# Two-layer sliding-window attention with gated MLP: the attention items' start, period and transposes in a hand-scheduled kernel

## The chip, the cores and the metric

The kernel runs on one core of a Trainium2 chip. The metric is the device time of one execution in microseconds (us). Engines are named as in the profile: PE (TensorE matmuls), PEld (its weight loads), DVE (VectorE), ACT (ScalarE), POOL (GpSimd), SP (the queue that issues weight transfers).

## What is computed

Two blocks run one after the other on a sequence of 512 tokens of width 1024. The first block (a pooling mixer and a gated recurrence) is not touched. The second block has two equal layers, and the change lies in these. Cut to what matters, one layer is:

```
for l in range(DEPTH):                                   # 2 layers
    h = x @ w_in[l] + b_in[l]
    q, k, v, z_a, u_g, v_g, z_g, g_a, g_g = split_columns(h)
    y_a = sliding_window_attention(q, k, v, attn_sinks[l]) * silu(z_a)
    y_g = chunked_spatial_gating(gelu(u_g), gelu(v_g), ...) * silu(z_g)
    merged = sigmoid(g_a) * (y_a @ w_branch_attn[l]) + sigmoid(g_g) * (y_g @ w_branch_gmlp[l])
    x = layer_norm(ALPHA * x + merged @ w_out[l] + b_out[l], ...)

# sliding_window_attention: blocks of 128 queries, keys of this block and the one before
scores = q k^T / 8 - slope * dist, masked;  m = max(scores.max(-1), sink)
p = exp(scores - m);  out = (p / (p.sum(-1) + exp(sink - m))) @ v
```

## The kernel before

All tensors are in SBUF with features on the partitions, 512 tokens along the free axis. Each projection is made from 256-column units of a weight. A float32 product is done as three matmuls of rounded parts: `hi` (a rounded copy, made by ACT in line 239) and `lo` (the remainder, made by DVE in line 245), and likewise `xhi` and `xlo` of the activations; so one 128-feature tile of a projection is 8 x 3 matmuls of 128x512 into a PSUM tile `pi` (line 319 is the one line that issues every matmul, line 323 every transpose).

The whole program is put in order by hand, while it is built. The main thread issues projections; beside it stand jobs (Python generators, list `sides`). After every few matmuls the main thread calls `tick()`, which gives each job in the list one step: what a step issues goes into the engines' queues at that place. A job that yields a number of microseconds is left alone until a counter of planned PE time (`clock`) has passed by that much. The engines run their queues strictly in that order, and semaphores hold an instruction until its operands are there.

A layer goes: `layer_head` (projections of k, v and q, six PSUM tiles, two of them the two-bank tiles `pj` of which there are two buffers in all), then `layer` with the evacuation of these tiles (`ev_kv`, `ev_q`, lines 1346 to 1381), the units u0 and u1 (GELU, line 1400), vg (GELU and a layer norm per 128 tokens, lines 1620 to 1631), za0 and za1, zg0 and zg1 (SiLU by Tanh), `mix`, the gates, branches and the output.

Attention runs beside u, vg, za and zg. It is eight items (four query blocks n, two key/value heads g) of each four query heads. `attention` first forces everything in `need` to be issued (the evacuation of k, v and q), then spawns an item, gives it its first step, and waits `ATT` us before the next one:

```
def start(at):                                   # called with "u0", "u1", "vg0", ...
    if at == ATT_AT:
        z["att"] = self.spawn(self.attention(l, qs, ks, vtok, z, need))
...
job = self.spawn(self.att_item(l, n, g, qs, ks, vtok, z, prev))
self.step(job)
yield ATT
```

An item (`att_item`, from line 1676) is: 8 score matmuls on PE into a `pj` tile (out of `ks`, the keys, and `H`, which here is `qs`, the queries); bias, maximum (DVE, lines 1698 to 1708); Exp on ACT (line 1715); normalisation on DVE (lines 1719 to 1723); `yield self.after(t0, ATT_P)`, that is, a pause until `ATT_P` us after the scores; then four or eight 128x128 transposes on PE into another `pj` tile (their operand is called `s`, the normalised rows); rounded copies of the transposes (ACT line 1739, DVE line 1743); a pause of `ATT_O`; the product with the values (`vtok`, "PV" below) on PE; copy out (ACT line 1758). The queries come from DVE line 1381: eight subtractions, `H_1282` (g = 0) and `H_1283` (g = 1) in turn, each over 64 partitions, and item 0 (g = 0) reads all four of `H_1282`.

Of the kernel before, what the change touches and what calls it, by code (L numbers as in the profile page):

```python
# [27 lines left out]
QCH = 388  # L28
QBUFS = 4
P3_SLOTS = 9  # L30
ATT = 9
ATT_P = 12
ATT_O = 5
ATT_AT = "u1"
WAITS = {"za": (1, 0), "u": (1, 0), "zg": (1, 1)}
COLS = 3
CONSTS = 8
# [28 lines left out]
class Net:  # L66
# [1261 lines left out]
    def layer(self, l, xt, cols):  # L1328
# [78 lines left out]
        def start(at):  # L1407
            if at == ATT_AT:
                z["att"] = self.spawn(self.attention(l, qs, ks, vtok, z, need))
# [252 lines left out]
    def attention(self, l, qs, ks, vtok, z, need):  # L1662
# [4 lines left out]
        for n in range(4):  # L1667
            for g in range(2):
# [3 lines left out]
                self.step(job)  # L1672
                yield ATT
        return outs

    def att_item(self, l, n, g, qs, ks, vtok, z, prev):
# [44 lines left out]
        for j in range(4):  # L1721
            s = ph[j // 2][:, j % 2, :]
            nc.vector.tensor_scalar(s, s, rd[:, j:j + 1], None, op0=ALU.mult)  # L1723
        yield self.after(t0, ATT_P)
        pts = []
# [154 lines left out]
```

## Time and profile before

| | before |
|---|---|
| three runs, median (lowest to highest) | 1653.32 us (1653.0 to 1653.61) |
| the profiled execution, its own time | 1654.04 us |
| its span | 1652.3 us |
| PE busy | 1628.9 us, 99% |
| DVE busy | 997.3 us, 60% |
| ACT busy | 600.9 us, 36% |
| POOL busy | 111.0 us, 7% |
| DMA, mean | 85 GB/s |
| mean granted TensorE clock | 0.997 of full |

Start times are counted from the first instruction of the span; the own time of the profiled execution also holds 1.7 us that lie around the span. Layer 0 of the second block runs from about 980 to 1308 us, layer 1 from there to the end. A matmul's duration in the profile is longer than the distance to the next one's start, since they are pipelined: what a matmul costs a full PE is the distance from its start to the next start.

### The profile page before, as it was taken

How to read it: one execution, taken by the hardware profiler on the slowest of the kernel's cores; microseconds unless marked ns; L12 is line 12 of the kernel's file. 1: busy time of each engine (PE TensorE's matmuls, PEld its weight loads, DVE VectorE, ACT ScalarE, POOL GpSimd, SP SyncE). 2: the span in 40 equal slices, each digit the busy share in tenths (PEclk: the TensorE clock that was granted, in tenths of full speed). 3: DMA queues.
4: the chain of work that ended last, by engine and by line, in shares of the span. 5: the costliest groups of instructions: out<-in, count | busy, mean ns of one | idle time of the engine just before them, and what ended most of it. 6: DMA issues, size and time to landing. Idle time of an engine off the chain costs nothing.

```text
span 1652.3 us, 25936 instructions
## 1 busy us (share of the span) xinstructions
PE 1628.9 (99%) x10726; PEld 1474.2 (89%) x10726; DVE 997.3 (60%) x1879; ACT 600.9 (36%) x996; POOL 111.0 (7%) x171
## 2 busy tenths in 40 slices
PE   8999999999999999999999999999999999999997
PEld 7999999989999898888999898978888899788886
DVE  6564647466666757567666756686424656873346
ACT  4432222244322223223222236564223355752221
POOL 4000000031000000000000010011000200010002
PEclk9999999999999999999999999999999999999999
DMA  5323222222221221221211232132325232232231
GB/s 189 103 81 99 84 96 86 94 78 82 65 77 52 77 66 63 77 77 58 86 62 63 66 109 85 44 103 79 100 77 153 71 102 65 77 99 91 92 102 51
DMA packets 124776, 139.67 MB, mean 85 GB/s; under 512 B 5217, under 2 KB 109809, under 8 KB 124658
## 3 DMA queue, kind: packets, MB, share of 16 engines
q1 hardware_dynamic: 122178, 131.88, 25.4%
q0 software_dynamic: 2304, 5.81, 1.2%
q8 instruction: 84, 1.38, 0.3%
q14 instruction: 34, 0.28, 0.1%
q10 hardware_dynamic: 176, 0.33, 0.1%
HBM read 135.90 MB, written 2.10 MB: 84 GB/s over the span
## 4 chain that ended last, share of the span: by engine, by line
PE 90%; DVE 6%; ACT 2%; issue 1%; POOL 1%; DMA 0%; DVEq 0%; ACTq 0%; POOLq 0%
PE pj L319 56%; PE pi L319 31%; PE pi L323 2%; DVE lo L245 1%; PE pj L323 1%; DVE s L1698 0%; ACT pj L1555 0%; ACT s L1715 0%; DVE mx L1704 0%; DVE h1tok L1550 0%; POOL ss L1558 0%; DVE h1tok L1565 0%; DVE s L1743 0%; POOL rs L361 0%; DVE s L1723 0%
## 5 line engine op out<-in xcount | busy, mean ns | idle before, releaser
L245 DVE TENSOR_TENSOR lo<-raw,hi 128x1024 fp32r<-128x1024 f32 (+1 forms) x260 | 296.7, 1171 | 153.4 <-ACT hi L239 153.1
L319 PE MATMUL pj<-xhi,hi 128*128 128x264 f32 (+2 forms) x1360 | 347.6, 311 | 0.7 <-ACT xhi L482 0.7
L319 PE MATMUL pj<-xlo,hi 128*128 128x264 f32 (+2 forms) x1360 | 340.3, 306 | 5.2 <-DVE xlo L783 2.3
L319 PE MATMUL pj<-xhi,lo 128*128 128x264 f32 (+2 forms) x1360 | 339.4, 305 | 0.0
L239 ACT CAST hi<-raw 128x1024 fp32r<-128x1024 f32 (+1 forms) x260 | 247.2, 996 | 170.4 <-PE pj L319 94.0
L319 PEld LDWEIGHTS pj<-xlo,hi 128*128 128x128 f32 x1360 | 227.0, 190 | 14.6 <-DVE xlo L783 2.7
L319 PEld LDWEIGHTS pj<-xhi,hi 128*128 128x128 f32 x1360 | 228.1, 190 | 11.2 <-ACT xhi L482 1.1
L319 PEld LDWEIGHTS pj<-xhi,lo 128*128 128x128 f32 x1360 | 227.0, 190 | 10.4
L319 PE MATMUL pi<-xhi,hi 128*128 128x512 f32 (+3 forms) x576 | 213.1, 370 | 0.0
L319 PE MATMUL pi<-xhi,lo 128*128 128x512 f32 (+3 forms) x576 | 210.8, 366 | 0.0
L319 PE MATMUL pi<-xlo,hi 128*128 128x512 f32 (+3 forms) x576 | 210.6, 366 | 0.0
L319 PEld LDWEIGHTS pi<-xhi,lo 128*128 128x128 f32 x576 | 108.4, 188 | 17.5
L319 PEld LDWEIGHTS pi<-xhi,hi 128*128 128x128 f32 x576 | 108.5, 188 | 17.1
L319 PEld LDWEIGHTS pi<-xlo,hi 128*128 128x128 f32 x576 | 108.5, 188 | 16.6
L319 PE MATMUL pj<-s,hi 128*128 128x264 f32 x640 | 104.1, 284 | 0.0
L1106 DVE TENSOR_TENSOR s<-s,s 128x264 f32<-128x264 f32 (+1 forms) x112 | 47.8, 427 | 82.2 <-PE pi L319 81.3
L319 PEld LDWEIGHTS pi<-qq,s 128*32 128x32 f32 (+5 forms) x1024 | 87.2, 161 | 7.4 <-issue 4.0
L319 PE MATMUL pi<-qq,s 128*32 128x32 f32 (+5 forms) x1024 | 89.7, 245 | 0.0
L319 PEld LDWEIGHTS pj<-s,hi 128*128 128x128 f32 x640 | 88.9, 188 | 0.0
L319 PE MATMUL pj<-hi,yA 128*128 128x512 f32 x256 | 71.6, 401 | 0.5
L361 POOL TENSOR_TENSOR rs<-ms,cst 128x4 f32<-128x4 f32 (+2 forms) x27 | 23.4, 868 | 696.7 <-DVE ms L1223 537.5
L319 PE MATMUL pj<-s,lo 128*128 128x264 f32 x320 | 65.3, 285 | 0.0
(262 smaller groups left out, 2365.2 us busy)
## 6 DMA issues: line engine op xcount, KB each, us to landing
raw<-in_hgrn_w_in_dram SPq DMA_DIRECT2D x64, 512.0 KB, 3.8
raw<-in_w_in_dram SPq DMA_DIRECT2D x60, 512.0 KB, 3.7
raw<-in_pool_w_in_dram SPq DMA_DIRECT2D x32, 512.0 KB, 3.7
raw<-in_pool_w_out_dram SPq DMA_DIRECT2D x16, 512.0 KB, 3.8
raw<-in_hgrn_w_out_dram SPq DMA_DIRECT2D x16, 512.0 KB, 3.6
raw<-in_w_in_dram SPq DMA_DIRECT2D x32, 256.0 KB, 3.2
raw<-in_w_out_dram SPq DMA_DIRECT2D x16, 512.0 KB, 4.7
raw<-in_pool_w_grp_dram SPq DMA_DIRECT2D x8, 512.0 KB, 4.0
```

The costliest lines, as they stand in the source:

```text
L239: nc.scalar.copy(a, r)
L245: eng.tensor_tensor(b, r, a.bitcast(F32), op=ALU.subtract)
L319: self.nc.tensor.matmul(out, w, x, start=start, stop=stop)
L323: self.nc.tensor.transpose(out, x, ident)
L361: self.nc.gpsimd.tensor_tensor(y, x, self.mhalf[:m, :n], op=ALU.pow)
L1106: nc.vector.tensor_tensor(kv[:, :, 0, :], kv[:, :, 0, :], cv[:, :, 1:2].to_broadcast([P, nb, w]), op=ALU.mult,)
```

## The change

The attention generator is begun one unit earlier (at u0 and not at u1), its items come every 11 us of planned time and not every 9, and an item's transposes are allowed 11 us after its scores and not 12.

```diff
-ATT = 9
-ATT_P = 12
+ATT = 11
+ATT_P = 11
 ATT_O = 5
-ATT_AT = "u1"
+ATT_AT = "u0"
```

Since the two numbers are now equal, and the generator stands ahead of its items in the list of jobs, the tick that spawns item n+1 (its scores) also lets item n go on (its transposes).

PE, layer 0, the first unit of u: a piece of the difference (`pi_10208` is u's first tile, `pi_10217` holds the transposes of v, `pj_10240` the scores of item 0, with the last column the output's shape).

```order
 L319 MATMUL pi_10208<-xhi_9632,lo_10104 128x512
 L323 MATMUL pi_10217<-cst_79,s_10181 128x128 x4
+L319 MATMUL pj_10240<-ks_10170,H_10175 128x128 x4
+L319 MATMUL pj_10240<-ks_10172,H_10175 128x128 x4
 L319 MATMUL pi_10208<-xhi_9632,hi_10103 128x512
 L319 MATMUL pi_10208<-xlo_9633,hi_10103 128x512
```

The scores of item 0 now stand behind the first six matmuls of u and four transposes; before, they stood after 54 matmuls of u. Layer 1 has the same order at its own u.

DVE, layer 0, the same place, the kernel after (`H_1282` and `H_1283` are the queries, `h1tok` the residual).

```order
L1381 TENSOR_TENSOR H_1282_10175<-s_1286_10183,H_1282_10175 64x512
L1381 TENSOR_TENSOR H_1283_10176<-s_1286_10183,H_1283_10176 64x512
L1381 TENSOR_TENSOR H_1282_10175<-s_1287_10187,H_1282_10175 64x512
L1381 TENSOR_TENSOR H_1283_10176<-s_1287_10187,H_1283_10176 64x512
L1381 TENSOR_TENSOR H_1282_10175<-s_1288_10191,H_1282_10175 64x512
L1381 TENSOR_TENSOR H_1283_10176<-s_1288_10191,H_1283_10176 64x512
L1381 TENSOR_TENSOR H_1282_10175<-s_1289_10195,H_1282_10175 64x512
L1381 TENSOR_TENSOR H_1283_10176<-s_1289_10195,H_1283_10176 64x512
L1391 SCALAR_TENSOR_TENSOR h1tok_4226<-h1tok_4226,H_1291_10203 128x1024
L1367 TENSOR_TENSOR vtok_1281_10174<-pi_1295_10217,vtok_1280_10173 128x512
L245 TENSOR_TENSOR lo_1275_10162<-raw_1260_9822,hi_1274_10161 128x1024
...
L1698 SCALAR_TENSOR_TENSOR s_1303_10263<-cst_93_695,pj_1298_10240 128x128 x2
```

Up to and with the eight subtractions (and the row of line 1391 behind them) DVE's queue has the same rows in the same order as before; only behind them have rows moved: item 0's own (line 1698 on) follow right here, five rows earlier than before.

PE, layer 0, a later place, before (`pj_1420` holds the scores of item 5, `pi_1421` the PV of item 3, `pj_1422` the transposes of item 4, `pi_1416` a tile of za).

```order
L319 MATMUL pj_1420_10991<-ks_1279_10172,H_1283_10176 128x256 x4
L319 MATMUL pi_1421_11000<-s_1410_10938,vtok_1280_10173 128x512
L319 MATMUL pi_1421_11000<-s_1410_10938,vtok_1281_10174 128x512
L319 MATMUL pi_1421_11000<-s_1411_10939,vtok_1280_10173 128x512
L319 MATMUL pi_1421_11000<-s_1412_10941,vtok_1280_10173 128x512
L319 MATMUL pi_1421_11000<-s_1412_10941,vtok_1281_10174 128x512
L319 MATMUL pi_1421_11000<-s_1413_10942,vtok_1280_10173 128x512
L323 MATMUL pj_1422_11007<-cst_3_79,s_1405_10915 128x128 x2
L323 MATMUL pj_1422_11007<-cst_3_79,s_1406_10918 128x128 x2
L319 MATMUL pi_1416_10971<-xhi_1232_9632,hi_1391_10837 128x512
```

and after, the scores of item 4 (`pj_1387`) with the transposes of item 3 (`pj_1388`) behind them:

```order
L319 MATMUL pj_1387_10830<-ks_1277_10170,H_1282_10175 128x256 x4
L319 MATMUL pj_1387_10830<-ks_1279_10172,H_1282_10175 128x256 x4
L323 MATMUL pj_1388_10839<-cst_3_79,s_1372_10701 128x128 x2
L323 MATMUL pj_1388_10839<-cst_3_79,s_1373_10704 128x128 x2
L323 MATMUL pj_1388_10839<-cst_3_79,s_1372_10701 128x128 x2
L323 MATMUL pj_1388_10839<-cst_3_79,s_1373_10704 128x128 x2
L319 MATMUL pi_1390_10849<-xhi_1232_9632,hi_1339_10493 128x512
```

The PV of item 3 no longer stands in this place: it now comes 30 projection matmuls later.

## Rows read from the trace of the kernel before

**Rows 1.** The page: the span, and the busy time of each engine.

```profile
span 1652.3 us, 25936 instructions
PE 1628.9 (99%) x10726; PEld 1474.2 (89%) x10726; DVE 997.3 (60%) x1879; ACT 600.9 (36%) x996; POOL 111.0 (7%) x171
```

**Rows 2.** PE's waits over the whole span: total us, times, longest.

```profile
PE pj L319 <- DVE xlo L1241: 2.3, 1, 2.3
...
PE pi L319 <- DVE s L1743: 1.6, 2, 0.8
```

**Rows 3.** The chain of waits in layer 0, its two ends: start us, us, what.

```profile
1044.39 1.15 PE pj L319 x8
...
1084.28 1.46 PE pj L323 x8
```

**Rows 4.** Timeline of PE, layer 0: start us, us, engine, line, tiles, shape, count.

```profile
1009.52 0.60 PE L323 MATMUL pi<-cst,s 128*128 128x128 f32 x4
1009.87 0.48 PE L319 MATMUL pi<-xhi,hi 128*128 128x512 f32 x1
...
1021.80 1.55 PE L319 MATMUL pj<-ks,H 128*128 128x128 f32 x8
1023.28 0.50 PE L319 MATMUL pi<-xhi,hi 128*128 128x512 f32 x1
```

**Rows 5.** Timeline of DVE, layer 0.

```profile
1011.66 5.71 DVE L1381 TENSOR_TENSOR H<-s,H 64x512 fp32r<-64x512 f32 x8
...
1031.64 0.87 DVE L1723 TENSOR_SCALAR s<-s,rd 128x128 f32<-128x128 f32 x4
```

**Rows 6.** DVE line 1381 over both layers.

```profile
L1381 DVE TENSOR_TENSOR H<-s,H x16: 684/686/689, 1011.7 to 1354.7; 64x512 fp32r<-64x512 f32 x16
```

**Rows 7.** Timeline of PE, then of DVE, layer 1, the first unit of u.

```profile
1347.93 0.48 PE L319 MATMUL pi<-xhi,hi 128*128 128x512 f32 x1
...
1349.72 5.71 DVE L1381 TENSOR_TENSOR H<-s,H 64x512 fp32r<-64x512 f32 x8
```

**Rows 8.** Timeline of PE: PV of item 3, transposes of item 4, layer 0.

```profile
1081.37 0.73 PE L319 MATMUL pi<-s,vtok 128*128 128x512 f32 x2
1082.92 1.20 PE L319 MATMUL pi<-s,vtok 128*128 128x512 f32 x4 [0.82 <-DVE s L1743]
1084.28 1.46 PE L323 MATMUL pj<-cst,s 128*128 128x128 f32 x8 [0.16 <-DVE s L1723]
1085.50 0.48 PE L319 MATMUL pi<-xhi,hi 128*128 128x512 f32 x1
```

**Rows 9.** Timeline of PE: the same place in layer 1.

```profile
1420.98 1.20 PE L319 MATMUL pi<-s,vtok 128*128 128x512 f32 x4 [0.82 <-DVE s L1743]
1422.34 1.46 PE L323 MATMUL pj<-cst,s 128*128 128x128 f32 x8 [0.16 <-DVE s L1723]
```

**Rows 10.** Timeline of PE between the two layers.

```profile
1305.84 0.28 PE L319 MATMUL pj<-xhi,hi 128*128 128x256 f32 x1
1308.37 0.39 PE L319 MATMUL pj<-xlo,hi 128*128 128x256 f32 x1 [2.25 <-DVE xlo L1241]
...
1309.78 0.38 PE L319 MATMUL pj<-xhi,hi 128*128 128x256 f32 x1
...
1312.30 1.49 PE L323 MATMUL pi<-cst,h1tok 128*128 128x128 f32 x8
1313.55 0.37 PE L319 MATMUL pj<-xhi,hi 128*128 128x256 f32 x1
```

**Rows 11.** Windows there: stretch, length, PE, PEld, DVE, ACT, POOL busy, granted clock, DMA.

```profile
1309.00:1310.00 1.00, 1.00 (x10) 1.00 (x10) 1.00 (x2) 0.00 (x0) 0.00 (x0) 0.91 0.00 0
1310.00:1311.00 1.00, 1.00 (x6) 1.00 (x6) 0.20 (x3) 0.65 (x1) 0.00 (x0) 0.50 0.00 0
...
1313.00:1314.00 1.00, 1.00 (x9) 1.00 (x8) 1.00 (x2) 1.00 (x3) 0.95 (x2) 0.89 0.00 0
1314.00:1315.00 1.00, 1.00 (x11) 1.00 (x10) 1.00 (x3) 1.00 (x3) 1.00 (x2) 1.00 0.00 0
```

## The prediction, made before the changed kernel was run

> **What bounds the kernel now.** I read the page first: PE is busy 1628.9 of 1652.3 us, DVE 60% and ACT 36% [rows 1]. So the question for any change of order is not how long the vector work takes, but where PE is held. PE's waits over the whole span are short: next to the start and the end of the program there are 2.3 us between the two layers, and two waits of 0.8 us, one per layer, on the lower halves of the transposed weights of attention (line 1743) [rows 2]. The chain of waits could mislead here: from 1045.54, where the scores of item 2 end, to 1084.28, where the transposes of item 4 begin, it runs through DVE and ACT alone, 38.7 us in each layer [rows 3]. It shows that the vector side of attention has no slack left at 1084, but all that PE loses by it is what the timeline of PE shows there: 0.82 us ahead of the PV of item 3 and 0.16 us ahead of the transposes of item 4, and the same in layer 1 [rows 8, 9]. Third, I read PE and DVE at the entry of a layer, where the change puts item 0: at 1009.87 PE goes from the transposes of v straight on with u [rows 4], while DVE works on the queries' lower halves, eight subtractions from 1011.66 on [rows 5].
>
> **The change part by part.**
>
> *The start at u0.* In PE's queue the eight scores of item 0 now stand behind the first six matmuls of u and the four transposes of v. PE gets there at 1009.87, as before [rows 4]. The scores need four of the eight subtractions of line 1381, the first, third, fifth and seventh. DVE's queue is the same as before up to these, so they come at the same time: eight in 5.71 us at 0.69 each [rows 5, 6] gives a distance of (5.71 - 0.69) / 7 = 0.717 us, so the seventh starts at 1011.66 + 6 x 0.717 = 1015.96 and ends at 1016.65. The first three scores slip in before that; five are left. Eight cost 1023.28 - 1021.80 = 1.48 us where they stood [rows 4], five cost 0.93, and u goes on at 1017.58. That is 7.71 us after 1009.87. The 1.48 us that the scores cost at their old place go away there, so the entry costs 6.2 us net. Layer 1: u goes on now at 1347.93, the eight subtractions start at 1349.72 [rows 7], the seventh ends at 1354.71, u goes on at 1355.64, again 7.71 less 1.48, 6.2 us. Nothing lies beside this hold to cover it: the other matmuls of u are queued on PE behind the scores, and PE issues matmuls in order (between the layers one late operand left PE empty for 2.25 us [rows 10]). Bounds: 5.8, if the five scores run at 0.11 each, and 6.9, if the eighth subtraction is waited for too. I take 6.2 per layer.
>
> *The period of 11 and the transposes at 11.* The removed stall: at 1081.37 six PV matmuls take until 1084.28, 2.91 us [rows 8]. At full pace one takes at most 0.23 (between 1009.87 and 1021.80 there are 48 projection matmuls, four transposes and one float32 product, some 0.9 us for these two [rows 4]), so six take 1.4, and 1.5 are lost; the eight transposes behind them take 1.22 against 0.70 to 0.87 (the four of v took 0.35 [rows 4]). So PE loses between 0.98 us (the idle time alone) and 1.9 us there per layer. In the new order the PV of an item stands 30 projection matmuls, nearly 7 us, behind its transposes, where before it could stand right behind the next scores, and items are wider apart; I let the stall go altogether and take 1.6 us per layer, nearer the upper end because PE pays from start to start.
>
> *What is late next.* With both numbers 11, an item's transposes stand behind the next item's scores, some 48 projection matmuls (11 us) behind its own. Item 0 now needs 1031.64 + 0.87 - 1023.28 = 9.2 us from the end of its scores to its last normalised row [rows 4, 5], with other DVE work in between, so the transposes find their rows done. Later items have 256 keys and share DVE and ACT with the GELU and layer norm of vg, but more projection matmuls stand between one item's scores and the next's than before. A new hold there is bounded by 0 and by the 0.98 us that the worst item pays today [rows 8]; I take 0, the nearer value, since the load per microsecond of PE falls. Three of the 22 activation table loads go; they are ACT's, off PE's path, and cost nothing. The weight loads on SP and the small POOL operations keep their order and move along with the steps that issue them; PE running later gives them more room, not less. PE's own work is the same: 6880 rows before and after. The last PV stands some dozen matmuls earlier than before, so the branch products, at the same place as before, find it done.
>
> *The clock.* Between the layers PE stood empty for 2.25 us, and from 1309.78 on the granted clock was at 0.50, the lower of its two levels (1.2 of 2.4 GHz), until 1313.2 [rows 10, 11]. In that stretch 12 matmuls took 2.52 us where 11 had just taken 1.41, a loss of 1.0, and eight transposes 1.25 against 0.70, a loss of 0.5: 1.5 us together. The new hold is near three times as long, and it is in each layer. Bounds: 0, if the clock stays up, and 3.0, if it stays low twice as long. I take 1.5 per layer, the one row there is.
>
> The Trainium skill (TensorE: Matmul & The Clock Gate, Terms) prices a throttled stretch as its length times one minus the granted share. By that the stretch of 3.4 us costs 1.7 us, and the sum would end 0.4 us higher; the row's smaller 1.5 is measured on part of the stretch, and I stay with it.
>
> *The sum.* Per layer 6.2 - 1.6 + 0 + 1.5 = 6.1 us, two layers 12.2 us. The profiled execution took 1654.04 us by itself, so it would take 1666.2; the median of the runs shown, 1653.32, stands 0.7 lower, and I predict on it: **1665.5 us**.
>
> **The rivals.**
>
> 1. *The clock stays up* through the hold. For it: three short scores run inside the hold, and the 0.98 us at 1082 cost little. Against it: the much shorter gap of 2.25 us was enough [rows 10, 11]. Then 6.2 - 1.6 = 4.6 per layer, 1662.5 us.
> 2. *The clock stays low for longer*, 3.0 us of loss per layer. For it: the hold is three times the gap seen. 6.2 - 1.6 + 3.0 = 7.6, 1668.5 us; with a new hold of 0.98 in each layer, 1670.5.
> 3. *Faster: the entry is covered.* If the subtractions of line 1381 were not what PE waits for, or came first on DVE, only the gain would be left: 1653.3 - 3.2 = 1650.1 us. It decides at 1.6 us: the seventh subtraction would have to end by 1011.5 or so, which is before the first one begins [rows 5]. Nothing in the changed queue of DVE moves it.
> 4. *No change: the vector chain sets the pace and gives the loss back.* If the chain of 38.7 us [rows 3] held PE by more than the idle time shows, 6 us gained in its start could return. It would need 6 us of lost PE time between 1045 and 1085; the timeline shows 1.0 to 1.9 [rows 8]. 1653.3 us.
>
> That the change does not do what it says is excluded by the order: the scores stand in u0, and transposes stand directly behind scores from item 0 on.
>
> **How the numbers follow.** My forecast 0.64; rival 1 0.18; rival 2 0.12; rivals 3 and 4 0.03 each. The range holds the forecast and rival 1 and most of rival 2: down to 1661.5 (rival 1 with the full 1.9 of gain, 1661.9), up to 1670. A measurement of this kernel can tell about 0.2%, 3.3 us, from no change: the forecast and rivals 1 and 2 are slower by more than that, 0.94 together; rival 4 is the same, 0.03; rival 3 is 3.2 us faster, at the edge of what can be told, and I count its 0.03 as faster.
>
> **What would show it.** In the profile after: PE idle for some 6 us in front of the scores of item 0, at about 1010 and, shifted by the loss of layer 0, in layer 1, released by DVE line 1381; lines 1381 at the same 1011.7; no wait of PE on line 1743 or 1723 in za; a second and third stretch at granted clock 0.50 just behind the two holds. I am wrong if PE passes item 0's scores with less than 3 us of idle time, if the stalls in za stay, or if PE is held by the transposes of items 2 to 5.

## The result, and the profile after

The changed kernel takes **1679.29 us** (median of four executions, 1677.69 to 1679.84); the kernel before, timed beside it, 1653.34. The ratio is 1.0153, 95% interval [1.0141, 1.0166]: slower by 26 us. The sign was predicted; the size was not. The forecast was 1665.5 us with a range up to 1670.0.

The page of the kernel after, its span and engines:

```profile
span 1677.2 us, 25928 instructions
...
PE 1639.2 (98%) x10726; PEld 1482.8 (88%) x10726; DVE 996.6 (59%) x1879; ACT 597.0 (36%) x993; POOL 110.7 (7%) x171
```

Beside [rows 1], PE and DVE have the same number of instructions, ACT three fewer, and the vector work is the same within 4 us; PE's busy time grows by 10 us only. So of the 25 us by which the span grew, some 15 are idle time of PE and some 10 are the same matmuls run more slowly. The list of PE's waits over the whole span (total, times, longest) names the idle time:

```profile
PE pj L319 <- ACT ks L1363: 6.9, 2, 3.5
PE pj L323 <- DVE s L1723: 6.3, 2, 3.2
PE pj L319 <- DVE H L1381: 4.0, 4, 1.1
```

The wait on line 1743 of [rows 2] is gone, and the wait on line 1381 is there, as predicted. The second line was not predicted: twice, once per layer, PE stands 3.2 us at transposes (line 323) because an item's rows are not yet normalised (line 1723).

**The entry.** PE, layer 0, at the first unit of u (start, duration, engine, line, operation, tiles, shape, count, and in brackets the idle time ahead and its releaser):

```profile
1010.04 0.60 PE L323 MATMUL pi<-cst,s 128*128 128x128 f32 x4
1014.10 0.59 PE L319 MATMUL pj<-ks,H 128*128 128x128 f32 x2 [3.46 <-ACT ks L1363]
1015.80 0.47 PE L319 MATMUL pj<-ks,H 128*128 128x128 f32 x1 [1.11 <-DVE H L1381]
1017.24 1.52 PE L319 MATMUL pj<-ks,H 128*128 128x128 f32 x5 [0.96 <-DVE H L1381]
1018.69 0.79 PE L319 MATMUL pi<-xhi,hi 128*128 128x512 f32 x1
...
1022.63 0.39 PE L319 MATMUL pi<-xhi,hi 128*128 128x512 f32 x1
```

and the work that it waits for, on DVE and on ACT:

```profile
1012.19 5.71 DVE L1381 TENSOR_TENSOR H<-s,H 64x512 fp32r<-64x512 f32 x8
```

```profile
1013.43 1.26 ACT L1363 CAST ks<-ks 64x512 fp32r<-64x512 f32 x2
```

This is the hold that was predicted: 2 + 1 + 5 scores that follow the first, third, fifth and seventh subtraction. The transposes of v end at 1010.39 (four take 0.35, [rows 4]), u goes on at 1018.69: 8.30 us, against the predicted 7.71. A second operand, the copies of the keys on ACT (line 1363), holds the first two scores until 1014.10; the prediction had not seen it, and it is covered by the subtractions. The eight subtractions start 1.80 us after the transposes' end, the same distance as before [rows 4, 5].

In the hold the granted clock falls, after PE has stood idle. Windows of the kernel after (each figure of the clock is a mean over stretches at its two levels, 1.2 and 2.4 GHz; length, busy time of PE, PEld, DVE, ACT and POOL, granted clock, DMA share, GB/s):

```profile
1010.00:1020.00 10.00, 4.47 (x16) 3.35 (x15) 9.67 (x14) 8.40 (x11) 0.00 (x0) 0.79 0.18 52
1020.00:1030.00 10.00, 10.00 (x42) 8.12 (x42) 9.60 (x20) 4.31 (x12) 1.10 (x1) 0.87 0.50 145
...
1120.00:1130.00 10.00, 6.81 (x30) 5.24 (x29) 6.27 (x18) 5.13 (x15) 1.50 (x2) 0.92 0.20 65
1130.00:1140.00 10.00, 10.00 (x37) 8.29 (x37) 5.72 (x6) 5.28 (x10) 3.51 (x2) 0.74 0.36 106
```

The nine matmuls of u from 1018.69 to 1022.63 take 3.94 us; at the full pace of 0.227 they would take 2.04. That is a loss of 1.9, and the five scores take 1.45 where the forecast had 0.93. Together 2.4 us at the entry of layer 0, where 1.5 was predicted.

The Trainium skill (TensorE: Matmul & The Clock Gate, Terms) prices a throttled stretch as its length times one minus the granted share. By the two windows that is, as an estimate, (0.21 + 0.13) x 10 = 3.4 us for this place. The rows show 2.4: part of the stretch fell into time in which PE waited anyway (it stood until 1017.24, and from 1015 to 1020 the granted clock is 0.57).

**The late hold.** PE at items 6 and 7, layer 0: scores of item 7, transposes of item 6, and then the transposes of item 7, the last:

```profile
1112.86 1.30 PE L319 MATMUL pj<-ks,H 128*128 128x256 f32 x8
1114.08 1.09 PE L323 MATMUL pj<-cst,s 128*128 128x128 f32 x8
...
1125.73 0.39 PE L319 MATMUL pi<-xhi,lo 128*128 128x512 f32 x1
1129.31 2.03 PE L323 MATMUL pj<-cst,s 128*128 128x128 f32 x8 [3.19 <-DVE s L1723]
1130.98 0.78 PE L319 MATMUL pi<-xhi,hi 128*128 128x512 f32 x1
...
1135.31 0.39 PE L319 MATMUL pi<-xlo,hi 128*128 128x512 f32 x1
```

From 1125.73 to 1129.31 are 3.58 us where one matmul needs 0.23. The eight transposes take 1.67 against 0.85 at 1114.08, and the ten matmuls to 1135.31 take 4.33 where 2.27 is the full pace. So this place costs 3.35 + 0.8 + 2.1 = 6.2 us in layer 0, more than the whole sum that had been forecast for a layer. In layer 1 the wait is the same, but only the first three matmuls behind it are slow, and by the same working the place costs 4.7 us:

```profile
1480.56 2.02 PE L323 MATMUL pj<-cst,s 128*128 128x128 f32 x8 [3.16 <-DVE s L1723]
```

Why item 7's rows are late is read from ACT and DVE in that stretch:

```profile
1109.43 0.69 ACT L1269 ACTIVATE s<-pi,cst 128x512 f32<-128x512 f32 x1 [6.17 <-PE pi L319]
...
1110.58 0.51 ACT L1715 ACTIVATE s<-s,nm 128x256 f32<-128x256 f32 x1
...
1112.65 1.13 ACT L353 CAST ya<-s 128x512 fp32r<-128x512 f32 x2
1113.68 2.00 ACT L239 CAST hi<-raw 128x1024 fp32r<-128x1024 f32 x2
...
1118.44 0.63 ACT L353 CAST ya<-s 128x512 fp32r<-128x512 f32 x1 [2.15 <-DVE s L1768]
...
1120.25 1.07 ACT L1739 CAST s<-pj 128x512 fp32r<-128x512 f32 x2
```

```profile
1107.33 0.17 DVE L1708 TENSOR_SCALAR nm<-nm 128x4 f32<-128x4 f32 x1
...
1117.72 0.69 DVE L1768 TENSOR_TENSOR s<-s,H 128x512 f32<-128x512 f32 x1
...
1121.35 1.29 DVE L1743 TENSOR_TENSOR s<-pj,s 128x512 fp32r<-128x512 f32 x2 [1.56 <-ACT s L1739]
...
1123.16 1.41 DVE L1698 SCALAR_TENSOR_TENSOR s<-cst,pj 128x256 f32<-128x256 f32 x4
...
1128.80 1.14 DVE L1723 TENSOR_SCALAR s<-s,rd 128x256 f32<-128x256 f32 x4
```

Read it backwards. Line 1723 at 1128.80 is 5.6 us behind line 1698, the first reading of the scores, and that distance is the softmax itself. But line 1698 comes at 1123.16, 9 us after the scores were done. Ahead of it on DVE stands line 1743 of item 6, which needs ACT's line 1739; that stands behind line 353, which waits for DVE's line 1768. Lines 1768, 353 and 355 are the gating of finished pairs of items by za. They can only begin when the fourth tile of za is there, at 1109, and the pairs that have waited for it then come in one heap. The same step also forces that tile's evacuation into the queues (`for job in z["zj"]: self.get(job)`). ACT stood 6.17 us in front of that tile (line 1269), while item 6's exponentials (line 1715), ready from 1107.5 on (line 1708 at 1107.33), stood behind it until 1110.58.

The Trainium skill (TensorE: Matmul & The Clock Gate, Architectural detail) says that the queues of ACT and DVE are strictly first in, first out. The trace agrees: in those 6.17 us ACT did nothing, and for the last 1.9 of them the exponentials stood ready behind the waiting instruction.

### The profile page after: what moved, and what is told of

It is laid out like the page before. It is cut to its first block, busy times and chain, and to the rows that moved or that the text cites. A ratio compares the mean times of both kernels' runs of the same rounds, so it can differ in the third digit from the quotient of the medians.

```text
span 1677.2 us, 25928 instructions
## 1 busy us (share of the span) xinstructions
PE 1639.2 (98%) x10726; PEld 1482.8 (88%) x10726; DVE 996.6 (59%) x1879; ACT 597.0 (36%) x993; POOL 110.7 (7%) x171
## 4 chain that ended last, share of the span: by engine, by line
PE 92%; DVE 5%; ACT 2%; issue 1%; POOL 1%; DMA 0%; DVEq 0%; ACTq 0%
PE pj L319 56%; PE pi L319 33%; PE pi L323 2%; PE pj L323 1%; DVE lo L245 1%; DVE H L1381 1%; ACT s L1715 0%; ACT pj L1555 0%; DVE h1tok L1550 0%; POOL ss L1558 0%; DVE h1tok L1565 0%; DVE xlo L783 0%; DVE ks L1355 0%; POOL rs L361 0%; DVE s L1723 0%
## 5 line engine op out<-in xcount | busy, mean ns | idle before, releaser
L319 PE MATMUL pi<-xhi,hi 128*128 128x512 f32 (+3 forms) x576 | 216.6, 376 | 0.0
```

Of the source, the lines that this page charges most:

```text
L319: self.nc.tensor.matmul(out, w, x, start=start, stop=stop)
```

## The experiments

Each time is set against the kernel before timed beside it on the same chip (1653.87, 1654.06 and 1653.95 us), and differences are to that. For the changed kernel the difference is +25.95.

The theories at the start: **A**, the entry hold and the late hold are independent, and the late one comes from transposes issued directly behind the next scores. **B**, the late hold follows from the early start. **C**, the vector queues are late all along, whatever the order.

### The two parts alone

Start at u0 with the old period and place of the transposes (e1_start_only):

```diff
-ATT = 11
-ATT_P = 11
+ATT = 9
+ATT_P = 12
```

> The change's start alone: begun at u0, but period 9 and transposes at 12 as before. Theory A (two holds of their own: one at the entry, 8.3 us from the transposes of v to u's next matmul, less 1.5 that the scores cost anyway, with some 2 us of low clock behind it; and one ahead of the last item's transposes, 3.3 us with 0.8 and 2 us of low clock, which comes from issuing transposes directly behind the next scores): only the entry is left, 2 x 8.8 over before, 1671 us (1669 to 1673), PE held by lines 1363 and 1381 for some 5.5 us per layer and by line 1723 for under 1 us. Rival B (the late hold follows from the entry: PE late against the vector queues): both holds stay, 1677 to 1680.

Measured: 1675.92 us (+22.05, ratio 1.0134 [1.0119, 1.0149]), between A and B. The entry is the same. The 3.2 us hold on line 1723 is not there; four short ones are (2.4 us in all, the longest 0.7), with waits of 0.5 and 0.6 in each layer on lines 1743 and 1739. The early start alone costs nearly all of the loss, but B, by which it would bring the late hold with it, is missed.

The period and the transposes at 11, start at u1 as before (e2_period_only):

```diff
-ATT_AT = "u0"
+ATT_AT = "u1"
```

> The change's period alone: 11 and 11, but begun at u1 as before. Theory A: no hold at the entry, the hold ahead of item 7's transposes stays (3.3 + 0.8 + some 2 of low clock, less the 1.9 of the stall in za that goes): 2 x 4.2 over before, 1662 us (1659 to 1664). Rival B: no entry, no late hold, and the old stall gone: 1650 to 1653.

Measured: **1649.98 us** (-3.89, ratio 0.9977 [0.9968, 0.9986]). Neither the stall of [rows 8, 9] nor any other wait of PE in attention is left in either layer. That refutes A and C, and B's number is met: transposes directly behind the next scores hold nothing by themselves. This kernel beats both others. By themselves the two parts give +22.05 and -3.89, together +25.95: some 7.8 us come only of the two together. The late hold of 3.2 us needs the early start and the new numbers together.

The same with the transposes 2 us of planned time further on, which the expectation calls two steps (e8_u1_p13):

```diff
-ATT_P = 11
-ATT_AT = "u0"
+ATT_P = 13
+ATT_AT = "u1"
```

> Period 11 with the start at u1 (1649.98 us with the transposes at 11), and the transposes two steps behind the next item's scores (13). If the longer period alone removes the stall on line 1743 and the place of the transposes matters little: 1649 to 1651 us. Rival: the transposes directly behind the scores are what removes it, since the PV follows them and gets its operands at a better time: the stall comes back, 1652 to 1654 us.

Measured: 1650.73 us (-3.33, ratio 0.9978 [0.9968, 0.9989]). Not to be told from the run before it: the longer period is what removes the old stall, and whether the transposes stand at 11 or 13 matters little.

### The late hold

All transposes later, start at u0 (e3_apart):

```diff
-ATT_P = 11
+ATT_P = 14
```

> As the change, but an item's transposes at 14 and not 11, so that they stand some 3 us behind the next item's scores, as before the change. Theory A: DVE then reads the next scores (line 1698) ahead of the copies of this item's transposes (line 1743), item 7's softmax starts in time, the late hold goes, the entry stays: 2 x (8.8 - 1.9) over before, 1667 us (1665 to 1671). Rival B: no change against the changed kernel, 1677 to 1680.

Measured: 1672.79 us (+18.92, ratio 1.0116 [1.0101, 1.0131]). The late hold is gone, but waits of 0.9 us on line 1739 take its place ahead of a PV, with 0.5 on line 1743 behind them. A's number and B's are both missed.

Only item 7's transposes later (e4_last_later):

```diff
-        yield self.after(t0, ATT_P)
+        yield self.after(t0, 16 if n == 3 and g == 1 else ATT_P)
```

> As the change, but the last item's transposes 16 us and not 11 us behind its scores, all else alike. Theory A: the late hold (3.3 us and the low clock behind it) is covered by 5 us of projection, the entry stays: 1667 us (1666 to 1670). Rival C (the late hold is only the first visible sign of vector queues that are late all along): the hold moves to the next place where PE needs them (PV of item 7, or mix), 1674 to 1680.

Measured: 1667.63 us (+13.76, ratio 1.0083 [1.0066, 1.01]). No wait on line 1723 is left among PE's waits, and the entry is unchanged. A's number is met; C's is not, for the hold moves to no other place. So the late hold with its low clock is worth 25.95 - 13.76 = 12.2 us, 6.1 per layer (the two profiled spans differ by 11.1). This says what the hold costs, not why item 7 is late.

For that, two causes were set against each other. First the gating was put later (e9_gate_later; `yield 20` is a pause of 20 us of planned time, which the expectations call 20 steps):

```diff
         while len(z["zj"]) < 4:
             yield
+        if n < 3:
+            yield 20
```

> The changed kernel (1679.3 us), its gating of the finished halves (lines 1768, 353, 355) put 20 steps later for the first three pairs of items; with it item 6's exponentials come ahead of the fourth za tile in ACT's queue. Theory G (the late hold of 3.2 us per layer comes from the gating steps that pile up on ACT and DVE when the fourth za tile is there): the hold goes, 1666 to 1668 us, as with the last item's transposes at 16. Theory Q (it comes from line 1739 of item 6 standing in ACT's queue behind line 1269 of the first zg tile, whose matmuls end some 3 us after item 6's transposes): line 1739 starts only 1.2 us earlier, some 2 us of the hold stay, 1673 to 1677 us.

Measured: 1670.48 us (+16.53, ratio 1.0103 [1.0087, 1.0118]). ACT, then DVE, then PE of this kernel in the same stretch:

```profile
1107.90 0.51 ACT L1715 ACTIVATE s<-s,nm 128x256 f32<-128x256 f32 x1 [4.27 <-DVE nm L1708]
...
1109.99 0.67 ACT L1269 ACTIVATE s<-pi,cst 128x512 f32<-128x512 f32 x1
...
1115.59 1.07 ACT L1739 CAST s<-pj 128x512 fp32r<-128x512 f32 x2 [0.56 <-PE pj L323]
```

```profile
1118.61 0.76 DVE L1698 SCALAR_TENSOR_TENSOR s<-cst,pj 128x256 f32<-128x256 f32 x2
...
1125.05 1.14 DVE L1723 TENSOR_SCALAR s<-s,rd 128x256 f32<-128x256 f32 x4
```

```profile
1126.32 1.03 PE L323 MATMUL pj<-cst,s 128*128 128x128 f32 x8
...
1146.84 1.16 PE L319 MATMUL pi<-wT,H 128*128 128x128 f32 x8 [1.68 <-DVE s L1651]
```

Line 1739 now starts when item 6's transposes are done, 4.7 us earlier than in the changed kernel, and the scores of item 7 are read 4.5 us earlier. Item 7's transposes run without a wait. Theory G is right on the hold: it goes when the heap of gating steps goes from in front of item 7. But the edit moves two things: with the heap goes the early evacuation of the fourth za tile, and item 6's exponentials now run ahead of line 1269. How much each of the two gives was not tried. Theory Q is refuted as the sole cause: the first zg tile stands ahead of line 1739 here too, and delays it by nothing. G's time is missed by 2.5 us, because the gating, now late, makes PE wait 1.7 us per layer for line 1651 in the branch: a hold moved, not only removed.

Then zg's evacuations were put later, with the gating where it was (e11_zg_later):

```diff
-WAITS = {"za": (1, 0), "u": (1, 0), "zg": (1, 1)}
+WAITS = {"za": (1, 0), "u": (1, 0), "zg": (3, 1)}
```

> The changed kernel with zg's evacuations two steps later, so that item 6's lines 1739 and 1743 stand ahead of the first zg tile on ACT and DVE; the gating stays where it was. Theory Q: line 1739 still stands behind line 353 at 1118.4, which waits for the gating on DVE, but line 1743 and the scores of item 7 come 1.2 to 1.9 us earlier; the hold shrinks from 3.2 to 1.3 to 2.0 us, 1673 to 1676 us. Theory G: the gating decides and is not moved; 0.6 us at most (line 1275, no longer ahead of the scores), 1677 to 1680 us.

Measured: 1671.10 us (+17.15, ratio 1.0105 [1.0088, 1.0121]); the hold is 1.46 us:

```profile
1128.28 1.46 PE L323 MATMUL pj<-cst,s 128*128 128x128 f32 x8 [1.46 <-DVE s L1723]
```

Q had the hold right and the time too high; G, which allowed 0.6 us, is missed. So what e9 moved is the larger part of what stood in front of item 7, and not the whole. What this takes away are the 1.8 us of lines 1269, 1273 and 1275 in front of item 7, a part of the same queue: the hold is shorter by just these (3.19 against 1.46 us).

Both edits together (e12_both):

> Both edits together, the gating 20 steps later and zg's evacuations two steps later. Both theories: line 1739 of item 6 runs right behind its transposes, at about 1115 and not at 1120.25; item 7's rows are normalised some 5 us earlier, the late hold goes, and the entry is all that is left: 1666 to 1669 us. If a hold of over 1 us stays, neither of the two is its cause.

Measured: 1668.62 us (+14.67, ratio 1.009 [1.0075, 1.0105]). The time is within the forecast, and line 1739 runs at 1114.86, as expected, but a hold of 0.68 us stays, and its cause is again a tile that ACT waits for with item 7's exponentials behind it:

```profile
1122.15 0.69 ACT L1269 ACTIVATE s<-pi,cst 128x512 f32<-128x512 f32 x1 [6.22 <-PE pi L319]
```

### The entry

Item 0 begun 7 us of planned time later within u0 (e5_delay; the expectations call these seven steps):

```diff
         prev = None
         outs = []
+        yield 7
```

> The changed kernel, with item 0 begun seven steps later within u0 (period 11 and transposes at 11 stay). All theories: the wait of PE on line 1381 at the entry goes, and the low clock behind it, about 9 us per layer (6.8 of hold, some 2.2 of matmuls at half pace). Theory A (the late hold on line 1723 at the last item comes from where the items of u0 stand against the GELU and layer norm, whatever the entry does): the late hold stays, 1660 to 1663 us. Theory B (the late hold follows from the entry hold or from the start before u1): it goes too, 1649 to 1652 us, as with the start at u1.

Measured: 1656.25 us (+2.19, ratio 1.0011 [1.0001, 1.002]), between A and B. The entry costs nothing any more, and item 7 is not held either. A hold of 1.43 us stands at item 5 instead. DVE, then PE:

```profile
1099.25 0.69 DVE L1275 SCALAR_TENSOR_TENSOR H<-s,H 128x512 f32<-128x512 f32 x1 [3.45 <-ACT H L1273]
...
1101.59 1.14 DVE L1724 TENSOR_SCALAR s<-s,rd 128x256 f32<-128x256 f32 x4
```

```profile
1102.00 2.08 PE L323 MATMUL pj<-cst,s 128*128 128x128 f32 x8 [1.43 <-DVE s L1724]
```

DVE waits 3.45 us for the fourth za tile ahead of the normalisation. So the hold stays near that tile, and the item that stands there is the one that is held. The same with the gating later (e13_delay_gate; the expectation says item 6, it is item 5):

> The start seven steps later within u0 (1656.25 us) with the gating 20 steps later. The hold left there, 1.43 us per layer with matmuls at half pace behind it, stood behind lines 1275 and 1769 on DVE, which waited for ACT's fourth za tile ahead of item 6's lines 1720 to 1724. In the new order the normalisation stands first. If that wait is the cause, it goes, and with it some 2.5 to 3.5 us per layer: 1649 to 1651 us, even with the start at u1 (1650.0). Rival: the hold moves to another item, 1653 to 1657 us.

Measured: 1656.76 us (+2.81, ratio 1.0016 [1.0007, 1.0025]). The rival is right. The hold goes from item 5 and comes back at item 6 (1.43 us, and 0.74 more at item 7), since DVE now waits 4.90 us before it reads that item's scores:

```profile
1109.08 1.42 DVE L1699 SCALAR_TENSOR_TENSOR s<-cst,pj 128x256 f32<-128x256 f32 x4 [4.90 <-PE pi L319]
```

The scores were done at about 1100.7; the release comes with a PV that starts at 1108.42. I take it that a buffer `s` is what DVE waits for, kept longer by the late gating; that was not tried.

The four subtractions that item 0 needs put first, on top of e4 (e6_g0_first_last_later; the other four became a job of their own behind them):

```diff
-            for g, h in enumerate(here):
-                nc.vector.tensor_tensor(
-                    qs[g][here[1 - g], j, :], q[h], qs[g][h, j, :].bitcast(F32), op=ALU.subtract
-                )
+            low(q, 0, j)
+            return q
...
+        need += [self.evac(ev_q1(job, j)) for j, job in enumerate(need[1:])]
```

> The changed kernel with the last item's transposes at 16 (1667.6 us before) and the four subtractions of line 1381 that item 0 needs put ahead of the other four. If PE waits for just the last of these four: it comes as the fourth of the eight and not as the seventh, 3 x 0.717 = 2.15 us earlier; the hold is 2.15 us shorter in each layer, 1663.3 us, and somewhat less again if the low clock is shorter too (1661 to 1664). Rival: PE waits for the evictions of the queries on ACT (line 1363) and the subtractions follow these one by one, so the order within them gives nothing: 1666 to 1668 us.

Measured: 1661.46 us (+7.40, ratio 1.0047 [1.0032, 1.0062]), 6.4 less than e4, 3.2 per layer. PE:

```profile
1014.07 1.77 PE L319 MATMUL pj<-ks,H 128*128 128x128 f32 x8 [3.46 <-DVE H L1385]
1015.76 0.79 PE L319 MATMUL pi<-xhi,hi 128*128 128x512 f32 x1
```

The hold ends 2.9 us earlier than in the changed kernel, and the low clock ends earlier too. What held u was indeed the last of the four subtractions, as the prediction had it. The gain is larger than 2.15 us per layer partly because the eight follow each other faster in this order, in 5.03 us and not 5.71:

```profile
1012.16 5.03 DVE L1385 TENSOR_TENSOR H<-s,H 64x512 fp32r<-64x512 f32 x8
```

The two copies of the keys on ACT (line 1363) end at 1014.02 and 1014.66 in this run, the fourth subtraction at 1014.65. So the two operands come together now, and subtractions put still earlier would meet the keys as the next limit; that is read from the trace and was not tried.

PE kept busy through the hold, on top of e4 (e7_busy_last_later; the 26 matmuls are work that the kernel does not need):

```diff
+        if n == 0 and g == 0:
+            c, xh = self.clock, self.x(0)[0]
+            pd = self.pi()
+            for _ in range(26):
+                self.mm(pd, xh[:, :P], xh, start=True, stop=True)
+            self.clock = c
```

> The changed kernel with the last item's transposes at 16 (1667.6 us before), and 26 matmuls of 128x512 added ahead of item 0's scores in each layer; they write a spare bank that nobody reads. They fill 26 x 0.227 = 5.9 us of a hold of 6.8 us, so they lengthen nothing by themselves. Theory: the half-pace matmuls behind the hold come from PE having stood idle; then the granted clock stays at its upper level in both layers, the five scores take 0.93 and not 1.45 us and u goes on at full pace: 2.5 to 3.5 us less per layer, 1661 to 1663 us. Rival: the pace behind the hold is low for another reason (late operands, the throttle's own time): 1667 to 1669 us.

Measured: 1662.82 us (+8.76, ratio 1.0053 [1.0038, 1.0068]): 26 matmuls more in each layer, and 5.0 us less than e4. PE, and the window:

```profile
1010.19 0.60 PE L323 MATMUL pi<-cst,s 128*128 128x128 f32 x4
1011.12 6.19 PE L319 MATMUL pi<-xhi 128*128 128x512 f32 x26 [0.33 <-ACT H L1376]
1017.15 1.16 PE L319 MATMUL pj<-ks,H 128*128 128x128 f32 x8
1018.24 0.50 PE L319 MATMUL pi<-xhi,hi 128*128 128x512 f32 x1
```

```profile
1010.00:1020.00 10.00, 9.67 (x48) 7.88 (x47) 9.67 (x14) 8.57 (x11) 0.00 (x0) 1.00 0.17 54
```

The granted clock stays at 1.00, and u goes on 18.24 - 10.54 = 7.70 us behind the transposes. The 26 matmuls end just as the last operand comes (the eight scores then run without a wait), so the length of this entry is in part set by their number. The low clock behind the hold comes from PE having stood idle, and it costs 2.5 us per layer at the entry.

## Why the prediction was wrong

The runs make a ladder from before to after, and each rung is one term. Per layer: e2 against before, -3.89 / 2; e7 against e2, (8.76 + 3.89) / 2; e4 against e7, (13.76 - 8.76) / 2; after against e4, (25.95 - 13.76) / 2. By the spread of the runs each is good to some 0.5 us. The order of the rungs is a choice: the gain in za, above all, was measured with the start at u1.

| term, us per layer | predicted | measured |
|---|---|---|
| entry hold, net | +6.2 | +6.3 |
| stall in za removed | -1.6 | -1.9 |
| low clock at the entry | +1.5 | +2.5 |
| "What is late next" | 0 | +6.1 |
| sum | +6.1 | +13.0 |

- **The entry hold was right**, in place, cause and size. In the changed kernel the five scores start at 1017.24, 6.85 us after the transposes, where the sum had 6.78; the rest of the difference to 8.30 us is the clock's. That e7, with the clock up, has 7.70 us against 7.71 is in part luck, since its 26 matmuls help to set it. The step "the first three scores slip in before that" held, though line 1363 keeps the first two back until 1014.10; that lies inside the hold.
- **The removed stall was right**, at the upper end of its bounds (1.9). It is the period's doing (e2, e8).
- **The clock term was mis-sized.** The step "I take 1.5 per layer, the one row there is" took its price from a gap of 2.25 us [rows 10, 11] that made 12 short matmuls and eight transposes slow. Behind the longer hold nine or ten matmuls of twice the width and five scores ran at half pace: 2.5, inside the bounds of 0 and 3.0.
- **The step that failed is "A new hold there is bounded by 0 and by the 0.98 us that the worst item pays today [rows 8]; I take 0".** The bound came from the old order, in which the items stood elsewhere against za and zg; the largest wait of an old order bounds nothing in a new one. The reason given, that the load per microsecond of PE falls, is true (DVE 60% and 59% of the span; from 1085 to 1130 us it is busy for 36.6 us before and 33.0 after) and does not bear on it: the lateness came from who stands ahead of whom in two queues at 1110 to 1123, not from load. The hold is 3.2 us of idle time in each layer, and 6.1 with the low clock behind it.
- The sentence that I would be wrong "if PE is held by the transposes of items 2 to 5" looked at the right kind of place and two items too early.

Rival 2 had the nearest time (1668.5, or 1670.5 with a new hold of 0.98). Rival 3's number, only the gain left, is met by e2 (1649.98 against 1650.1), but not in rival 3's way: e2 leaves the early start out, and the entry was never covered.

Shown by runs: the four terms, that the late hold needs the early start (e2) and the new numbers (e1), that it goes with the gating heap and the za tile which that heap forces into the queue (e9), and that zg's evacuations are a smaller part of it (e11). Read from the trace alone: the way through ACT's lines 1269, 353 and 1739. Not settled: how much of it is the heap and how much the early place of the za tile, and what makes DVE wait in e13.

## What to carry to other kernels

When a stream of items is moved against other streams, follow the last items too, and write down for each engine which instruction at that place waits for another stream's tile, and what ready work stands behind it. A bound on a new wait has to come from the new order; the largest wait of the old one is not a bound. And price a hold of PE with what it makes slow behind it: here 6.3 us of hold cost 8.8, and 3.3 cost 6.1.

## What the runs showed of the hardware

Whether the clock falls behind a short wait is not fixed by the wait. In e5 the same transposes wait 1.43 us in both layers. In layer 0 the granted clock falls (the six matmuls from 1103.74 to 1106.37 take 0.44 us each, near half pace, and the window below is a mean of both levels), in layer 1 it stays at 1.00, the upper level. Of the six waits of 1.42 to 1.46 us in e5, e11 and e13, one in each layer, this is the only one behind which it fell. Windows behind the wait in layer 0 and in layer 1 of e5:

```profile
1105.00:1110.00 5.00, 5.00 (x20) 4.05 (x20) 4.97 (x11) 1.42 (x3) 0.00 (x0) 0.87 0.63 165
...
1445.00:1450.00 5.00, 5.00 (x24) 4.14 (x23) 4.93 (x12) 1.08 (x3) 0.13 (x1) 1.00 0.71 187
```

And work that nobody needs can pay: 52 matmuls more (e7) made the program 5.0 us faster than without them, since they kept the clock up through a hold that was there anyway.
